# Six of eleven feed-forward blocks by seven products in place of five, without a pause between them

## The chip, the cores and the metric

The kernel runs on one core of a Trainium2 chip. The metric is the device time of one execution in microseconds. The engines are TensorE (PE), VectorE (DVE), ScalarE (ACT) and GpSimd (POOL); SyncE (SP) here only issues DMAs.

## The reference, cut to what matters

Three layers run one after the other on 256 tokens of width 2048, each with its norm and its mixer, all in float32. The change touches the feed-forward part of the first layer, of hidden width 5632:

```
h2 = rms_norm(x, norm2_g)                                   # 256 x 2048
x = x + (silu(h2 @ w_gate) * (h2 @ w_up)) @ w_down          # 2048 x 5632 twice, 5632 x 2048
```

## The kernel before

Float32 products are made from three matmuls each: an operand is split into a rounded part `hi` (a cast on ScalarE, L162) and the rest `lo` (a subtraction on VectorE, L163), and `three` (L186 to L189) multiplies hi by hi, hi by lo and lo by hi. Every weight tile (128 x 2 x 512, 512 KB) is loaded, split, and used once. `raw` tiles have five buffers, `hi` and `lo` four each.

The hidden width is cut into 11 blocks of 512. A block is done in one of two ways:

- `plain(j)`: `linear` for w_gate, then for w_up, each 8 weight tiles against the whole of h2; silu on the first, the scaling and product at L556, then `act_done`: transposes on TensorE (`tr`, L545) and a split, which leave the block's activations in the form that the down product multiplies with.
- `seven(j)`: a scheme with seven products of half-size matrices in place of eight. It queues 28 side pieces in `side`. A piece loads a tile, forms what it multiplies, splits it, and issues 6 matmuls (`times`). The first 12 pieces (`first`: three products) take raw tiles as loaded; the later 16 (`rest`: four products, b5, b7, b6 and b4) take differences of block tiles, made at L668 on VectorE. Block tiles (`b`, and two `u` units) live in a ring of six buffers and are loaded by `ahead` one step before they are used. The last piece calls `last`: additions on VectorE (L676 to L682) that combine the products, silu (L297, L298), two scalings (L685), and `act_done`.

The side pieces run between the matmuls of the main work. After each `three` of a `linear`, `deal` counts one, and when `pace[0]` deals have passed it issues the next piece. `down(bs, last)` multiplies the activations of blocks `bs` by w_down, four column blocks of 512 one after the other, and adds each into x on VectorE (`x_add`, L254, two additions).

Before, plain block 0 comes first, then five rounds, each with one seven block queued beside one plain block and one down call of two blocks; `drain` issues what is left of the queue at the end of each round. All weight loads are issued by SP (`rows`, L126), in one queue. A scheduler puts each engine's instructions in a fixed order when the kernel is built; at run time each engine takes its own in that order and waits on semaphores.

Of the kernel before, what the change touches and what calls it, by code (L numbers as in the profile page):

```python
# [18 lines left out]
P = 128  # L19
# [61 lines left out]
def model(ctx, tc, a, out):  # L81
    nc = tc.nc
# [14 lines left out]
    def nm(s):  # L97
        cnt[0] += 1
        return f"{s}{cnt[0]}"
# [4 lines left out]
    def unit(i, shape, dtype=F32):  # L104
        return wk.tile([P] + list(shape), dtype, tag=f"u{i}", name=nm(f"u{i}_"))
# [15 lines left out]
    def raw_tile():  # L121
        return raw_p.tile([P, 2, 512], F32, tag="raw", name=nm("raw"))

    def rows(dst, w, k, c0, n=512):

        nc.sync.dma_start(dst[:, :, :n], w[k * P:(k + 2) * P, c0:c0 + n].rearrange("(k p) f -> p k f", p=P))  # L126

    def fetch(w, kg, c0, n):

        raws = [raw_tile() for _ in range(2)]  # L130
        for i in range(2):
            rows(raws[i], w, 4 * kg + 2 * i, c0, n)
        return raws
# [26 lines left out]
    def split(hi, lo, src, scale=None):  # L160
        if scale is None:
            A.copy(hi, src)  # L162
            V.tensor_tensor(lo, src, hi.bitcast(F32), ALU.subtract)  # L163
        else:
            A.activation(hi, src, AF.Copy, scale=scale)
            V.scalar_tensor_tensor(lo, src, scale, hi.bitcast(F32), ALU.mult, ALU.subtract)
# [9 lines left out]
    side = deque()  # L176
    pace = [1, 0]

    def deal():
        if side:  # L180
            pace[1] += 1
            if pace[1] >= pace[0]:
                pace[1] -= pace[0]
                side.popleft()()

    def three(o, xh, xl, hi, lo, start, stop):  # L186
        T.matmul(o, xh, hi, start=start, stop=False)  # L187
        T.matmul(o, xh, lo, start=False, stop=False)  # L188
        T.matmul(o, xl, hi, start=False, stop=stop)  # L189

    def linear(w, c0, n, groups, got=(), fine=False):
        accs = [ps_acc.tile([P, 512], F32, tag="acc", name=nm("acc")) for _ in range(2)]
        for gi, ((xh, xl), kg) in enumerate(groups):
            raws = got[gi] if gi < len(got) else fetch(w, kg, c0, n)
            for k in range(4):
                k2 = k % 2
                if k2 == 0:
                    raw = raws[k // 2]
                    hi = hl_p.tile([P, 2, 512], F32R, tag="hi", name=nm("hi"))
                    lo = hl_p.tile([P, 2, 512], F32R, tag="lo", name=nm("lo"))  # L200
                    if fine and gi == 0:
                        for j in range(2):
                            split(hi[:, j, :n], lo[:, j, :n], raw[:, j, :n])
                    else:
                        split(hi[:, :, :n], lo[:, :, :n], raw[:, :, :n])
                for t in range(2):
                    o = accs[t][:, :n]
                    st, en = gi == 0 and k == 0, gi == len(groups) - 1 and k == 3
                    sl = slice(t * P, (t + 1) * P)
                    three(o, xh[:, k, sl], xl[:, k, sl], hi[:, k2, :n], lo[:, k2, :n], st, en)  # L210
                    deal()
        return accs
# [35 lines left out]
    def full(st):  # L248
        return [(st["T"][b], b) for b in range(4)]

    def x_add(b, accs):
        for t in range(2):
            xs = x[:, t, b * 512:(b + 1) * 512]
            V.tensor_tensor(xs, xs, accs[t], ALU.add)  # L254
# [61 lines left out]
    for b in range(4):  # L316
        xh, xl = st["T"][b] = pair(xt_p, "x")
# [13 lines left out]
    got = first  # L331
    for c0, n in ((2688, 400), (2304, 384), (2048, 256)):
        accs = linear(w_in, c0, n, full(st), got, fine=n == 400)
        got = []
# [91 lines left out]
    for vb in range(2):  # L426
# [4 lines left out]
        for hh in range(2):  # L431
# [19 lines left out]
            for t in range(2):  # L451
                o = po[:, t * S:(t + 1) * S]
                T.matmul(o, aT[:, t], v[:, t, vs], start=True, stop=True)
                for c in range(2):
                    n = 2 * t + c
# [69 lines left out]
    w_gate, w_up, w_down = a["w_gate"][0], a["w_up"][0], a["w_down"][0]  # L525
# [3 lines left out]
    acts = {}  # L529
    nst = new_stream()  # L530

    def down(bs, last):
        for b in range(4):
            x_add(b, linear(w_down, b * 512, 512, [(acts[j], j) for j in bs]))
            if last:
                x_done(nst, b, NEV)

    def act_done(j, sg):
        ah, al = acts[j] = pair(mt_p, "m")
        for i in range(2):  # L540
            ps = ps_w.tile([P, 512], F32, tag="w", name=nm("tr"))
            for k in range(2):
                for t in range(2):
                    c = (2 * i + k) * P
                    T.transpose(ps[:, k * S + t * P:k * S + (t + 1) * P], sg[:, t, c:c + P], ident)  # L545
            split(ah[:, 2 * i:2 * i + 2].rearrange("p c s -> p (c s)"),
                  al[:, 2 * i:2 * i + 2].rearrange("p c s -> p (c s)"), ps)

    def plain(j):
        ag = linear(w_gate, j * 512, 512, full(st))  # L550
        sg = unit(4, [2, 512])
        for t in range(2):
            silu_gate(sg[:, t], ag[t], rh[:, t:t + 1])
        au = linear(w_up, j * 512, 512, full(st))
        for t in range(2):
            V.scalar_tensor_tensor(sg[:, t], au[t], r2h[:, t:t + 1], sg[:, t], ALU.mult, ALU.mult)  # L556
        act_done(j, sg)

# [63 lines left out]
    def work_bank():  # L624
        return ps_w.tile([P, 512], F32, tag="w", name=nm("at"))

    def seven(j):

        c0 = j * 512
        c = {}  # L630

        def first(kp, n):
            if kp == 0:
                c[n] = work_bank()
            raw = raw_tile()
            rows(raw, (w_gate, w_up, w_gate)[n], (0, 8, 8)[n] + 2 * kp, c0)
            times(c[n], ("A11", "S4", "A12")[n], parts(raw), kp)
            if n == 2:
                ahead(0, kp)
            if kp < 3:  # L640
                return
            if n < 2:
                c["p", n] = temp("Lx", 4)
                A.copy(c["p", n], c[n])
                return
            sg = c["sg"] = unit(5, [2, 512])
            c11 = temp("junk2", 3)
            V.tensor_tensor(c11, c["p", 0], c[2], ALU.add)
            silu_gate(sg[:, 0], c11, rh[:, 0:1])

        def ahead(kp, n):

            if kp > 3:
                return
            for i in ((0, 1), (), (2,), (3,))[n]:
                b = c["b", kp, i] = block_tile()
                rows(b, (w_up, w_gate, w_up, w_gate)[i], (0, 0, 8, 8)[i] + 2 * kp, c0)

        def rest(kp, n):
            ahead(kp + 1, n)  # L660
            if n == 0:
                if kp == 0:
                    pace[0] = 5.75
                    c["P"] = [work_bank() for _ in range(3)] + [ps_acc.tile([P, 512], F32, tag="acc", name=nm("acc"))]
            b12, b11, b22, b21 = [c["b", kp, i] for i in range(4)]
            dst, x0, x1, which = ((b11, b12, b11, "S1"), (b12, b22, b12, "S3"), (b22, b22, b11, "S2"),
                                  (b21, b22, b21, "A22"))[n]
            V.tensor_tensor(dst, x0, x1, ALU.subtract)  # L668
            times(c["P"][n], which, parts(dst), kp)
            if kp == 3 and n == 3:  # L670
                last()

        def last():
            b5, b7, b6, b4 = c["P"]
            p1, p3, sg = c["p", 0], c["p", 1], c["sg"]
            V.tensor_tensor(p1, p1, b6, ALU.add)  # L676
            c12, c21 = temp("junk2", 3), temp("junk2", 3)
            V.tensor_tensor(c12, p1, b5, ALU.add)
            V.tensor_tensor(p1, p1, b7, ALU.add)
            V.tensor_tensor(c21, p1, b4, ALU.subtract)  # L680
            V.tensor_tensor(p1, p1, b5, ALU.add)
            V.tensor_tensor(c12, c12, p3, ALU.add)  # L682
            silu_gate(sg[:, 1], c21, rh[:, 1:2])
            for t, cu in enumerate((c12, p1)):
                V.scalar_tensor_tensor(sg[:, t], cu, r2h[:, t:t + 1], sg[:, t], ALU.mult, ALU.mult)  # L685
            act_done(j, sg)


        pace[0] = 1.75
        side.extend([lambda kp=kp, n=n: first(kp, n) for kp in range(4) for n in range(2)])  # L690
        side.extend([lambda kp=kp: first(kp, 2) for kp in range(4)])
        side.extend([lambda kp=kp, n=n: rest(kp, n) for kp in range(4) for n in range(4)])

    def drain():
        while side:
            side.popleft()()
        pace[0] = 1

    plain(0)
    left_sums()  # L700
    for w in range(5):
        seven(2 * w + 1)
        plain(2 * w + 2)
        down([2 * w - 1, 2 * w + 2] if w else [0, 2], False)
        drain()
    down([9], True)
    st = nst
    r, rh, r2 = stats(st)

# [72 lines left out]
    for half in range(2):  # L782
# [15 lines left out]
        for c in range(4):  # L798
            i = 4 * half + c
# [202 lines left out]
    for g in range(4):  # L1002
# [4 lines left out]
        sg = unit((0, 4)[g % 2], [2, 512])  # L1007
# [53 lines left out]
```

## Time and profile before

| | |
|---|---|
| three timed runs | 1927.04, 1927.17, 1930.02 us; median 1927.17 |
| the profiled execution | 1926.19 us, its span 1924.4 us |
| busy share of the span | PE 99%, DVE 66%, ACT 50%, POOL 10% |
| granted TensorE clock | 1.00 of full speed |
| feed-forward stage | about 446 to 1140 us of the span |

Times in the views count from the start of the span. A matmul's listed time includes its way through the array, so that neighbours overlap; the step from start to start is what one costs. In brackets behind a row stands the time for which the engine stood idle before it, and what ended that.

### The profile page before, as it was taken

The numbers are of one execution on the slowest core, as the hardware profiler recorded it, in microseconds if no ns is written. First come the engines' busy times: TensorE is split into PE (matmuls) and PEld (weight loads), VectorE is DVE, ScalarE is ACT, GpSimd is POOL, SyncE is SP. The second block draws the span as 40 slices with busy tenths as digits, with TensorE's granted clock in tenths as the row PEclk, the third lists the DMA queues.
The fourth block names the chain that finished last, engine by engine and source line by source line (L and its number), as shares of the span: only waits on it lengthen the run. The fifth ranks groups of instructions, "written<-read, shape, count | busy, mean of one in ns | idle before, by whom it ended". The sixth has DMA issues, their size and how long they took to land.

```text
span 1924.4 us, 23805 instructions
## 1 busy us (share of the span) xinstructions
PE 1906.0 (99%) x8808; PEld 1567.0 (81%) x8808; DVE 1276.6 (66%) x1486; ACT 968.9 (50%) x1313; POOL 201.1 (10%) x315
## 2 busy tenths in 40 slices
PE   8999999999999999999999999999999999999999
PEld 8877888888778888788787888888888888878787
DVE  6454555587787887787887875555555666677654
ACT  6544545465546546455455454444444354566542
POOL 1000222110000000000000110100000003754100
PEclk9999999999999999999999999999999999999999
DMA  8675665567768778677687656566666556544464
GB/s 306 198 209 152 186 175 165 166 207 249 247 223 276 233 227 272 221 259 240 229 268 238 191 165 192 159 196 169 191 188 191 191 179 188 170 132 132 146 202 134
DMA packets 202724, 387.72 MB, mean 201 GB/s; under 512 B 12312, under 2 KB 20528, under 8 KB 202480
## 3 DMA queue, kind: packets, MB, share of 16 engines
q1 hardware_dynamic: 201472, 382.12, 64.3%
q0 software_dynamic: 992, 4.03, 0.7%
q8 instruction: 69, 1.13, 0.2%
q14 instruction: 47, 0.39, 0.1%
q10 hardware_dynamic: 144, 0.05, 0.0%
HBM read 384.04 MB, written 3.68 MB: 201 GB/s over the span
## 4 chain that ended last, share of the span: by engine, by line
PE 89%; DMA 4%; DVE 4%; issue 1%; POOL 1%; ACT 0%; SPq 0%; DVEq 0%; ACTq 0%
PE acc L188 25%; PE acc L187 25%; PE acc L189 25%; PE at L188 2%; PE at L189 2%; PE at L187 2%; DVE lo L163 2%; DMA b<-in_w_up_dram 2%; DMA b<-in_w_gate_dram 1%; PE at L960 1%; DVE b L668 1%; DMA u<-in_w_up_dram 1%; PE tr L225 1%; PE tr L307 1%; DMA u<-in_w_gate_dram 0%
## 5 line engine op out<-in xcount | busy, mean ns | idle before, releaser
L163 DVE TENSOR_TENSOR lo<-raw,hi 128x1024 fp32r<-128x1024 f32 (+3 forms) x646 | 786.4, 1224 | 464.8 <-ACT hi L162 460.2
L162 ACT CAST hi<-raw 128x1024 fp32r<-128x1024 f32 (+3 forms) x646 | 669.4, 1040 | 664.8 <-PE acc L189 561.5
L188 PE MATMUL acc<-lo,xh 128*128 128x512 f32 (+3 forms) x1640 | 637.2, 389 | 0.4 <-DVE lo L163 0.4
L189 PE MATMUL acc<-hi,xl 128*128 128x512 f32 (+3 forms) x1640 | 636.2, 388 | 0.0
L187 PE MATMUL acc<-hi,xh 128*128 128x512 f32 (+3 forms) x1640 | 622.7, 390 | 5.7 <-ACT hi L162 5.7
L187 PEld LDWEIGHTS acc<-hi,xh 128*128 128x128 f32 x1640 | 308.2, 188 | 68.8 <-ACT hi L162 6.0
L188 PEld LDWEIGHTS acc<-lo,xh 128*128 128x128 f32 x1640 | 308.9, 188 | 64.1 <-issue 3.3
L189 PEld LDWEIGHTS acc<-hi,xl 128*128 128x128 f32 x1640 | 309.0, 188 | 59.5 <-issue 0.4
L188 PE MATMUL acc<-lo,mh 128*128 128x512 f32 x640 | 251.0, 392 | 0.0
L189 PE MATMUL acc<-hi,ml 128*128 128x512 f32 x640 | 249.0, 393 | 0.0
L187 PE MATMUL acc<-hi,mh 128*128 128x512 f32 x640 | 247.1, 393 | 1.0 <-ACT mh L162 1.0
L187 PEld LDWEIGHTS acc<-hi,mh 128*128 128x128 f32 x640 | 120.5, 188 | 27.1 <-DVE x L254 1.5
L188 PEld LDWEIGHTS acc<-lo,mh 128*128 128x128 f32 x640 | 120.3, 188 | 25.7 <-DVE lo L163 1.8
L189 PEld LDWEIGHTS acc<-hi,ml 128*128 128x128 f32 x640 | 119.8, 188 | 24.4
L162 ACT CAST hi<-b 128x1024 fp32r<-128x1024 f32 x54 | 56.9, 1054 | 74.5 <-PE acc L189 47.3
L163 DVE TENSOR_TENSOR lo<-b,hi 128x1024 fp32r<-128x1024 f32 x54 | 65.9, 1221 | 4.8 <-ACT hi L162 3.9
L668 DVE TENSOR_TENSOR b<-b,b 128x1024 f32<-128x1024 f32 x41 | 50.1, 1222 | 28.3 <-DMA b<-in_w_gate_dram 13.5
L720 POOL DMA_DIRECT2D u<-in_c_even_dram x1 | 0.6, 633 | 651.9 <-PE at L189 651.9
L254 DVE TENSOR_TENSOR x<-x,acc 128x512 f32<-128x512 f32 x88 | 57.7, 681 | 9.9 <-PE acc L189 9.8
L188 PE MATMUL at<-lo,u 128*128 128x512 f32 x160 | 63.5, 397 | 0.4 <-DVE lo L163 0.3
L189 PE MATMUL at<-hi,u 128*128 128x512 f32 x160 | 62.4, 390 | 0.0
L187 PE MATMUL at<-hi,u 128*128 128x512 f32 x160 | 62.4, 390 | 0.0
(253 smaller groups left out, 1567.1 us busy)
## 6 DMA issues: line engine op xcount, KB each, us to landing
raw<-in_ev_w_in_dram SPq DMA_DIRECT2D x128, 512.0 KB, 3.9
raw<-in_w_gate_dram SPq DMA_DIRECT2D x88, 512.0 KB, 4.5
raw<-in_w_down_dram SPq DMA_DIRECT2D x88, 512.0 KB, 5.1
raw<-in_w_in_dram SPq DMA_DIRECT2D x80, 512.0 KB, 3.8
raw<-in_od_w_in_dram SPq DMA_DIRECT2D x72, 512.0 KB, 3.7
raw<-in_w_up_dram SPq DMA_DIRECT2D x68, 512.0 KB, 4.7
raw<-in_w_out_dram SPq DMA_DIRECT2D x32, 512.0 KB, 3.6
raw<-in_ev_w_out_dram SPq DMA_DIRECT2D x32, 512.0 KB, 3.7
```

Of the source, the lines that this page charges most:

```text
L162: A.copy(hi, src)
L163: V.tensor_tensor(lo, src, hi.bitcast(F32), ALU.subtract)
L187: T.matmul(o, xh, hi, start=start, stop=False)
L188: T.matmul(o, xh, lo, start=False, stop=False)
L189: T.matmul(o, xl, hi, start=False, stop=stop)
L225: T.transpose(ps[:, k * S + t * P:k * S + (t + 1) * P], x[:, t, c:c + P], ident)
L254: V.tensor_tensor(xs, xs, accs[t], ALU.add)
L307: T.transpose(ps[:, k * S + t * P:k * S + (t + 1) * P], src(t)[:, c:c + P], ident)
L668: V.tensor_tensor(dst, x0, x1, ALU.subtract)
L720: nc.gpsimd.dma_start(ce, a["c_even"][:, :512])
L960: T.matmul(pv[e * 64:(e + 1) * 64, :S], vo[:, k, g * 64:(g + 1) * 64], PT[:, :, e], start=k == 0, stop=k == t)
```

## The change

The six seven blocks are 1, 3, 5, 7, 9 and 10; 0, 2, 4, 6 and 8 stay plain. All six are queued at once after block 0, and side pieces run on without a drain between them, at pace 1.5 in the first 12 pieces of a block and 4.85 in its later 16 (4.1 for block 1), where 1.75 and 5.75 stood; `drain` comes once, before the last down call. There are seven down calls in place of six. Block tiles are loaded by GpSimd's queue, in program order. `plain` hands back its `act_done`, which is called by `linear` behind the first group of the next down call's first column block (`mid`). Lines move by 3 up to `plain` (L163 stays, L254 becomes L257, L298 L301, L545 L548, L556 L559) and by 6 in `seven` (L668 becomes L674, L676 to L682 become L682 to L688, L685 L691).

```diff
-    def rows(dst, w, k, c0, n=512):
+    def rows(dst, w, k, c0, n=512, queue=nc.sync):
-        nc.sync.dma_start(dst[:, :, :n], w[k * P:(k + 2) * P, c0:c0 + n].rearrange("(k p) f -> p k f", p=P))
+        return queue.dma_start(dst[:, :, :n], w[k * P:(k + 2) * P, c0:c0 + n].rearrange("(k p) f -> p k f", p=P))
...
     def deal():
         if side:
             pace[1] += 1
-            if pace[1] >= pace[0]:
+            while side and pace[1] >= pace[0]:
                 pace[1] -= pace[0]
                 side.popleft()()
...
-    def linear(w, c0, n, groups, got=(), fine=False):
+    def linear(w, c0, n, groups, got=(), fine=False, mid=None):
         accs = [ps_acc.tile([P, 512], F32, tag="acc", name=nm("acc")) for _ in range(2)]
-        for gi, ((xh, xl), kg) in enumerate(groups):
+        for gi, (pr, kg) in enumerate(groups):
+            if gi == 1 and mid is not None:
+                mid()
+            xh, xl = pr() if callable(pr) else pr
...
-    def down(bs, last):
+    def down(bs, last, mid=None):
         for b in range(4):
-            x_add(b, linear(w_down, b * 512, 512, [(acts[j], j) for j in bs]))
+            x_add(b, linear(w_down, b * 512, 512, [(lambda j=j: acts[j], j) for j in bs], mid=mid if b == 0 else None))
...
-        act_done(j, sg)
+        return lambda: act_done(j, sg)
...
             if kp == 0:
+
+                pace[0] = 1.5
                 c[n] = work_bank()
...
-                rows(b, (w_up, w_gate, w_up, w_gate)[i], (0, 0, 8, 8)[i] + 2 * kp, c0)
+                tc.keep_in_program_order(rows(b, (w_up, w_gate, w_up, w_gate)[i], (0, 0, 8, 8)[i] + 2 * kp, c0,
+                                              queue=nc.gpsimd))
...
-                    pace[0] = 5.75
+                    pace[0] = 4.85 if j > 1 else 4.1
...
-        pace[0] = 1.75
...
-    plain(0)
+    plain(0)()
     left_sums()
-    for w in range(5):
-        seven(2 * w + 1)
-        plain(2 * w + 2)
-        down([2 * w - 1, 2 * w + 2] if w else [0, 2], False)
-        drain()
-    down([9], True)
+    for j in (1, 3, 5, 7, 9, 10):
+        seven(j)
+    mid = plain(2)
+    down([0], False)
+    mid()
+    down([2, 1], False)
+    for j in (4, 6, 8):
+        mid = plain(j)
+        down([j - 1, j], False, mid)
+    down([9], False)
+    drain()
+    down([10], True)
```

SP's order before, where the up product of plain block 2 is loaded; `raw` tiles of w_up belong to it, `b` tiles to block 1, which runs beside it:

```order
L126 DMA raw852_4141<-in_w_up_dram 128x2x512
L126 DMA raw863_4202<-in_w_up_dram 128x2x512
L126 DMA b860_4189<-in_w_gate_dram 128x2x512
L126 DMA raw864_4203<-in_w_up_dram 128x2x512
L126 DMA raw873_4253<-in_w_up_dram 128x2x512
L126 DMA b855_4157<-in_w_up_dram 128x2x512
L126 DMA raw874_4254<-in_w_up_dram 128x2x512
L126 DMA b869_4232<-in_w_up_dram 128x2x512
```

The same place of SP's order after:

```order
L126 DMA raw858_4167<-in_w_up_dram 128x2x512
L126 DMA raw869_4228<-in_w_up_dram 128x2x512
L126 DMA raw870_4229<-in_w_up_dram 128x2x512
L126 DMA raw881_4290<-in_w_up_dram 128x2x512
L126 DMA raw882_4291<-in_w_up_dram 128x2x512
L126 DMA raw893_4352<-in_w_up_dram 128x2x512
```

And the first block loads in GpSimd's order after, with nothing between them:

```order
L126 DMA b811_3973<-in_w_up_dram 128x2x512
L126 DMA b812_3975<-in_w_gate_dram 128x2x512
L126 DMA b819_4010<-in_w_up_dram 128x2x512
L126 DMA b827_4038<-in_w_gate_dram 128x2x512
L126 DMA u10_830_4048<-in_w_up_dram 128x2x512
```

The block loads have left the places between raw loads and are a sequence of their own.

TensorE's order before, where the transposes of a plain block (`tr`, L545) stand; `mh` and `ml` are activations in a down product (accumulator `acc`), `at` a product of the seven block:

```order
L188 MATMUL acc1325_6410<-lo1332_6433,mh1175_5720 128x512
L189 MATMUL acc1325_6410<-hi1331_6432,ml1176_5721 128x512
L187 MATMUL at1262_6098<-hi1335_6444,u3_763_3789 128x512
L545 MATMUL tr1323_6396<-cm_90,u4_1276_6163 128x128
L187 MATMUL acc1326_6411<-hi1329_6416,mh1175_5720 128x512
L188 MATMUL acc1326_6411<-lo1330_6417,mh1175_5720 128x512
```

And after, at a plain block's transposes in a later down product:

```order
L188 MATMUL at1384_6580<-lo1477_7044,u2_761_3785 128x512
L189 MATMUL at1384_6580<-hi1476_7043,u8_762_3786 128x512
L548 MATMUL tr1480_7064<-cm_90,u4_1421_6771 128x128 x4
L187 MATMUL at1385_6581<-hi1486_7093,u2_761_3785 128x512
L188 MATMUL at1385_6581<-lo1487_7094,u2_761_3785 128x512
```

Four transposes stand together now, later in the down product, among a side piece's matmuls.

VectorE's order before at the end of block 1, from the first addition of `last` up to its first scaling; `at836` is product b6, `lo` tiles from `raw` belong to the down product:

```order
L676 TENSOR_TENSOR c802_3944<-c802_3944,at836_4070 128x512
L163 TENSOR_TENSOR lo970_4739<-raw967_4734,hi969_4738 128x1024
L678 TENSOR_TENSOR c959_4694<-c802_3944,at834_4068 128x512
L163 TENSOR_TENSOR lo972_4755<-raw968_4735,hi971_4754 128x1024
L679 TENSOR_TENSOR c802_3944<-c802_3944,at835_4069 128x512
L682 TENSOR_TENSOR c959_4694<-c959_4694,c806_3961 128x512
L254 TENSOR_TENSOR x_91<-x_91,acc939_4595 128x512
L668 TENSOR_TENSOR b1047_5081<-b1046_5079,b1047_5081 128x1024
L254 TENSOR_TENSOR x_91<-x_91,acc940_4596 128x512
L163 TENSOR_TENSOR lo976_4775<-raw973_4770,hi975_4774 128x1024
L685 SCALAR_TENSOR_TENSOR u5_830_4053<-c959_4694,r2h694_3443,u5_830_4053 128x512
```

And after, the same end of block 1 (`at834` is b6 there), up to the lo tile lo959 of the down product that follows; the first scaling comes two rows later:

```order
L682 TENSOR_TENSOR c800_3931<-c800_3931,at834_4054 128x512
L163 TENSOR_TENSOR lo942_4591<-raw930_4532,hi941_4590 128x1024
L163 TENSOR_TENSOR lo946_4601<-raw944_4598,hi945_4600 128x1024
L684 TENSOR_TENSOR c935_4554<-c800_3931,at832_4052 128x512
L674 TENSOR_TENSOR b1011_4865<-b1010_4863,b1011_4865 128x1024
L163 TENSOR_TENSOR lo950_4620<-raw948_4617,hi949_4619 128x1024
L163 TENSOR_TENSOR lo953_4635<-raw951_4632,hi952_4634 128x1024
L685 TENSOR_TENSOR c800_3931<-c800_3931,at833_4053 128x512
L688 TENSOR_TENSOR c935_4554<-c935_4554,c804_3951 128x512
L257 TENSOR_TENSOR x_91<-x_91,acc927_4529 128x512
L257 TENSOR_TENSOR x_91<-x_91,acc928_4530 128x512
L163 TENSOR_TENSOR lo959_4653<-raw956_4648,hi958_4652 128x1024
```

More lo subtractions of 1024 elements stand between the additions than before: those of the next seven block's first products (lo946, lo950, lo953) have joined the down product's.

## Rows read from the trace of the kernel before

**Rows 1.** The page, engines: busy us, share of the span, instructions.

```profile
PE 1906.0 (99%) x8808; PEld 1567.0 (81%) x8808; DVE 1276.6 (66%) x1486; ACT 968.9 (50%) x1313; POOL 201.1 (10%) x315
```

**Rows 2.** Windows: stretch, length, engines' busy us; then PE clock, DMA share, GB/s.

```profile
446.00:1140.00 694.00, 687.27 (x3065) 561.98 (x3064) 554.43 (x556) 369.29 (x400) 12.18 (x30) 1.00 0.74 237
...
590.00:618.00 28.00, 28.00 (x125) 23.19 (x124) 19.63 (x18) 17.33 (x18) 0.00 (x0) 1.00 0.91 295
```

**Rows 3.** Timeline of PE, two neighbours: start us, us, engine, line, operation.

```profile
565.57 0.39 PE L188 MATMUL at<-lo,u 128*128 128x512 f32 x1
565.80 0.39 PE L189 MATMUL at<-hi,u 128*128 128x512 f32 x1
```

**Rows 4.** Waits, 446 to 1140: us in all, times, longest; then PE's timeline.

```profile
PE tr L545 <- DVE u L556: 5.3, 4, 1.9
...
528.14 0.39 PE L187 MATMUL at<-hi,u 128*128 128x512 f32 x1
530.48 0.33 PE L545 MATMUL tr<-cm,u 128*128 128x128 f32 x1 [1.95 <-DVE u L556]
```

**Rows 5.** Timeline of DVE at two plain blocks' scalings.

```profile
528.53 1.23 DVE L668 TENSOR_TENSOR b<-b,b 128x1024 f32<-128x1024 f32 x1 [3.29 <-DMA b<-in_w_gate_dram]
529.67 1.40 DVE L556 SCALAR_TENSOR_TENSOR u<-acc,r2h,u 128x512 f32<-128x512 f32 x2
...
785.09 1.23 DVE L668 TENSOR_TENSOR b<-b,b 128x1024 f32<-128x1024 f32 x1 [2.98 <-DMA b<-in_w_gate_dram]
```

**Rows 6.** Waits, 446 to 1140, of DVE and of SP's queue.

```profile
DVE b L668 <- DMA b<-in_w_gate_dram: 13.2, 5, 3.3
...
SPq L126 <- DVE lo L163: 540.0, 304, 6.9
```

**Rows 7.** Timeline of DVE at the end of block 1.

```profile
563.57 1.23 DVE L668 TENSOR_TENSOR u<-b,u 128x1024 f32<-128x1024 f32 x1 [2.39 <-DMA b<-in_w_up_dram]
...
570.51 0.68 DVE L676 TENSOR_TENSOR c<-c,at 128x512 f32<-128x512 f32 x1
571.11 1.22 DVE L163 TENSOR_TENSOR lo<-raw,hi 128x1024 fp32r<-128x1024 f32 x1
572.24 0.68 DVE L678 TENSOR_TENSOR c<-c,at 128x512 f32<-128x512 f32 x1
...
578.78 0.74 DVE L685 SCALAR_TENSOR_TENSOR u<-c,r2h,u 128x512 f32<-128x512 f32 x1
579.44 0.68 DVE L680 TENSOR_TENSOR c<-c,acc 128x512 f32<-128x512 f32 x1
```

**Rows 8.** Timeline of PE, block 1's first transposes.

```profile
581.77 0.38 PE L545 MATMUL tr<-cm,u 128*128 128x128 f32 x2
```

**Rows 9.** Timeline of POOL and DVE, issues and operations of POOL.

```profile
1072.80 0.55 POOL L721 DMA_DIRECT2D u<-in_c_even_dram  x1
1072.86 1.23 DVE L163 TENSOR_TENSOR lo<-raw,hi 128x1024 fp32r<-128x1024 f32 x1 [0.36 <-ACT hi L162]
...
1083.89 1.23 DVE L163 TENSOR_TENSOR lo<-raw,hi 128x1024 fp32r<-128x1024 f32 x1
1084.11 1.20 POOL L839 TENSOR_TENSOR tabs<-co__9133 128x64 f32<-128x64 f32 x1
...
1085.69 0.32 POOL L839 TENSOR_TENSOR tabs<-co__9133 128x64 f32<-128x64 f32 x1
1085.76 0.69 DVE L679 TENSOR_TENSOR c<-c,at 128x512 f32<-128x512 f32 x1
```

**Rows 10.** DMA issues, 446 to 1140: count, KB each, median us to landing.

```profile
raw<-in_w_down_dram SPq DMA_DIRECT2D x88, 512.0 KB, 5.1
...
b<-in_w_gate_dram SPq DMA_DIRECT2D x25, 512.0 KB, 4.7
...
u<-in_c_even_dram POOLq DMA_DIRECT2D x1, 512.0 KB, 5.1
...
co__9133<-in_od_sinks_dram POOLq DMA_DIRECT2D x1, 16.0 KB, 5.3
```

## The prediction

> **What bounds the kernel now.** I read the engine table first: TensorE is busy 1906.0 of 1924.4 us, VectorE 66%, ScalarE 50% [rows 1]. A gain has to come from fewer matmuls or from TensorE's few idle microseconds, and nothing else can shorten the span. The windows view then separates the feed-forward stage from the rest: in its 694 us TensorE is busy 687.27 and VectorE 554.43, or 80%, at granted clock 1.00; in a stretch where a seven block's first products run, the DMA share is 0.91 at 295 GB/s [rows 2]. So VectorE and the DMA engines are the ones with little left there, ScalarE is not (369 of 694).
>
> The timeline of TensorE gives the unit of the sum. Three 512-column matmuls start 0.227 us apart, though each is listed with 0.39, since they are pipelined [rows 3]. The view of waits names where the stage's idle time sits: TensorE waits 5.3 us in four places for the scaling at L556, in front of a plain block's activation transposes (L545) [rows 4]. From start to start each place loses 0.16 more (0.39 less 0.227), so 5.3 + 4 x 0.16 = 5.9 us.
>
> Why the scaling is late stands in VectorE's timeline: it stood 3.29 us at L668, a seven block's subtraction, until a block tile of w_gate had landed, and only then came to L556; 257 us later the same stands there with 2.98 [rows 5]. Block tiles land late because SP's queue issues in order: it waits 540.0 us in 304 places for a raw buffer that VectorE must finish with, and block loads stand behind those waits [rows 6].
>
> **The change part by part.** *Fewer matmuls.* A plain block has two products of 4 groups x 4 slices x 2 row halves x 3 = 192 matmuls; a seven block 7 x 8 x 3 = 168. Block 10 changes kind: 24 x 0.227 = 5.4 us less on TensorE, which sets the end. The number of down matmuls is the same.
>
> *Transposes moved.* In the changed order 25 to 54 matmuls (at least 5.6 us) stand between the up product's last matmul and the plain transposes, where 18 (4.1 us) stood. A stall like that of rows 5 fits under them, all the more if block tiles come earlier. I take all 5.9 us as gained; the other end is none of it, if VectorE's stall grows by as much.
>
> *Block loads on GpSimd's queue.* 96 loads (80 before) leave SP and are alone on their queue through the stage, in program order; SP's raw loads no longer have them in between. Each waits only for its own buffer, which the order frees four side pieces or more ahead: a piece is 4.85 x 3 + 6 = 20.6 matmuls, 4.66 us, so 18.6 us ahead, and at pace 4.1 16.6 us. A 512 KB load from GpSimd landed in 5.1 us, a block load from SP in 4.7 [rows 10]. That leaves 11.5 us to spare, so I price this at nothing; what hides it is the ring of six tiles, and without that cover each late load would stop VectorE as in rows 5. Issuing costs GpSimd 0.55 us, and one such issue lay under a running lo subtraction without growing [rows 9].
>
> GpSimd's tensor operations do suffer beside VectorE: the same operation took 0.32 us beside L679, which reads PSUM, and 1.20 beside a lo subtraction, whose operands all lie in SBUF [rows 9]. The Trainium skill (SBUF — State Buffer, "SBUF: two separate sides") has a rule against this part of the change: while VectorE runs a two-port operation, GpSimd cannot write the descriptors of its own DMAs, and a load of about 0.62 us took about 3.1. By that rule, an estimate from the page's two figures, each load would come 2.5 us later; within 11.5 us of spare the sum would be the same, and only if VectorE leaves no gaps would it be rival D. The one issue of rows 9 that lies beside VectorE does not show the rule.
>
> *Six blocks without a pause.* A seven block's VectorE work is 28 lo subtractions and 16 block subtractions at 1.13 us, and about 13 short ones at 0.60 to 0.66, together 58 us; a plain block's is 16 x 1.13 + 6 short = 22 us (pitches from rows 7). One block more of the first kind, one less of the second, and 8 residual adds of the seventh down call give 36 + 5 = 41 us: 595 in some 690, 86%. While block 1's later products run (pace 4.1, down of one block) a piece holds 2.27 + 1.16 + 0.6 = 4.0 us of VectorE work in 4.15 us. That covers nothing that comes late, so the ends of the six seven blocks decide.
>
> *Block ends.* When the last matmul of product b6 is done, VectorE runs L676 and its followers, and TensorE transposes what the two scalings (L685) leave. Before, 11 operations, 4 of them long, go up to the first scaling: 7 x 0.61 + 4 x 1.13 = 8.8 us, and TensorE has 68 matmuls (15.4 us) until its transposes: 6.6 us over. The trace agrees: L676 began 4.3 us after the matmul that began at 565.80 had ended, since VectorE had waited 2.39 us for a block tile just before; the scaling ended at 579.52, and the transposes began at 581.77, without a wait [rows 7, 8].
>
> After, the pieces come closer and the down products' own subtractions and residual adds stand among the same operations. For block 1 the order puts 12 operations (6 long) up to lo959, which TensorE wants 33 matmuls after b6: 10.4 us of work against 7.5 us. The same count for the others, work up to the scaling against matmuls up to its transposes: block 3, 9.3 against 42 (9.5 us); block 5, 11.7 against 43 (9.8); block 7, 10.0 against 58 (12.7); block 9, 9.3 against 42 (9.5); block 10, second scaling, 14.3 against 68 (15.2). The balances are -2.9, +0.2, -1.9, +2.7, +0.2 and +0.9.
>
> Something comes on top of each: the last matmul's 0.39 us, 0.07 from the scaling to the transposes, and the rest of the operation VectorE is in, half of 1.13. That is 1.1 us, and with it TensorE waits 4.0 + 0.9 + 3.0 + 0 + 0.9 + 0.2 = **9.0 us**. Bounds: nothing, if the scheduler's places leave more room than my count; and 26.6 us (7.2 + 4.1 + 6.2 + 1.6 + 4.1 + 3.4), if VectorE gets to L676 4.3 us late as in rows 7. I take a value near the low end, because the cause of those 4.3 us, a block load behind SP's waits, is what moves.
>
> *First products' pace.* At 1.5 in place of 1.75 a piece takes 10.5 matmuls, not 11.25, so the demand goes from 295 to 303 GB/s and the DMA share from 0.91 to about 0.93. Raw loads still fit; their failure is in D. Outside the stage the order hardly moves: no cost.
>
> Sum against the profiled execution's 1926.2: -5.4 - 5.9 + 9.0 = 1923.9. That execution is 1.0 below the median of the three runs (1927.17), so on the runs' scale I say **1925 us**. A measurement of this kernel can tell 0.2% (3.9 us) from no change.
>
> **Rivals.** *B, block ends cost nothing.* For it: before, the same ends had 2.2 us left over even with VectorE 4.3 us late. Against it: five of six counts have under 1 us of spare. Time: 1926.2 - 11.3 = 1914.9, 1916 on the runs' scale.
>
> *C, VectorE becomes the bound at the ends (slower).* It reaches L682 (the former L676) about 4.3 us after b6 at each end, because at 86 to 97% load it no longer runs ahead. Place: the transposes at L548 and the first down matmuls after them. Price 26.6 us, so 1926.2 - 11.3 + 26.6 = 1941.5, 1942 on the runs' scale. It decides the sign as soon as the ends cost more than 11.3 us together, 1.9 us each. For it: the load; against it: in the old order VectorE's waits for block loads, not its load, made the lateness.
>
> *D, the new queue does not help.* GpSimd's loads come late, or take DMA time from SP's raw loads in the stretches at 0.91, where four block loads and the first products' raw loads overlap. If two queues halve the rate there, a raw load of 5.1 us takes 2.5 more at each of six phases: +15, so 1938.9, 1940 on the runs' scale. For it: a 16 KB load from GpSimd took 5.3 us, no less than 512 KB [rows 10]. Against it: 11.5 us of spare. The rule on descriptors named above would give this case its cause.
>
> **How the numbers follow.** My forecast (ends cost 5 to 15 us) 0.57; B 0.18; C 0.14; D 0.11. The forecast's own range is 1921 to 1931. Faster by over 0.2% means under 1923.3: all of B and about a third of the forecast (ends under 7.5 us), 0.38. Slower, over 1931.0: nearly all of C, most of D, 0.22. The rest, 0.40, is within. The range runs from B at its least, 1915, up to 1935, which leaves out C and D at full price, less than 2 in 10 after what falls short of it.
>
> **What would show it.** Right: TensorE's matmul count 24 lower at the same clock; no wait of L548 on L559 (the former L556); new waits of L548 on L691 (the former L685) and of L188 on lo near blocks 1 and 5, 3 to 4 us each; VectorE's waits for block tiles (13.2 us for one kind in rows 6) mostly gone. Wrong: waits at all six ends over 3 us (C); VectorE still waiting for block DMAs, or GpSimd loads landing in over 8 us (D); no wait over 1 us at any end (B). The step I trust least is the 1.1 us.

## The result, and the profile after

The changed kernel takes 1971.25 us (median of four runs, 1968.65 to 1978.41), against 1927.11 for the kernel before: slower by the factor 1.0235 (95% interval 1.0221 to 1.0249). I had said 1925 us, 1915 to 1935.

The engine table of the profiled execution, which answers to [rows 1]:

```profile
span 1966.9 us, 23847 instructions
...
PE 1914.1 (97%) x8784; PEld 1566.1 (80%) x8784; DVE 1316.3 (67%) x1529; ACT 983.4 (50%) x1327; POOL 275.8 (14%) x411
```

The span is 42.5 us longer. TensorE's idle time went from 18.4 us to 1966.9 - 1914.1 = 52.8, so 34.4 us are waits. The other 8.1 are longer busy time with 24 matmuls fewer; as those took 5.4 us with them, the matmuls that are left cost 13.5 us more. The windows view shows a part of that, here around the end of block 1 (columns as in [rows 2]):

```profile
560.00:570.00 10.00, 5.06 (x20) 3.36 (x18) 10.00 (x12) 3.15 (x3) 0.00 (x0) 0.91 0.70 211
570.00:580.00 10.00, 9.06 (x35) 7.02 (x36) 7.10 (x9) 3.40 (x5) 0.00 (x0) 0.75 0.39 115
580.00:590.00 10.00, 10.00 (x49) 8.34 (x48) 9.45 (x11) 7.41 (x10) 0.00 (x0) 1.00 0.79 265
```

The timeline of TensorE at the same place:

```profile
569.76 0.80 PE L187 MATMUL acc<-hi,mh 128*128 128x512 f32 x1 [2.73 <-DVE x L257]
571.49 0.79 PE L188 MATMUL acc<-lo,mh 128*128 128x512 f32 x1 [0.94 <-DVE lo L163]
572.08 0.63 PE L189 MATMUL acc<-hi,ml 128*128 128x512 f32 x1
572.51 0.63 PE L188 MATMUL acc<-lo,mh 128*128 128x512 f32 x1
```

TensorE waits again and again from 560 to 571 us, busy 5.06 of 10, while VectorE is busy all 10.00. After it the granted clock falls to 0.75 as a mean of the next 10 us: the last two matmuls start 0.43 us apart, not 0.227 [rows 3], so they run at the lower of the clock's two levels, 1.2 and not 2.4 GHz. By 580 it is whole again. The granted clock is at half like this in four stretches of the execution, the first of them ahead of the feed-forward stage:

```profile
431.60:435.10 3.50, 3.46 (x8) 2.78 (x9) 3.50 (x4) 1.04 (x1) 0.00 (x0) 0.51 0.50 150
568.10:575.00 6.90, 4.31 (x9) 3.10 (x10) 6.55 (x10) 0.72 (x1) 0.00 (x0) 0.51 0.68 222
684.20:691.10 6.90, 5.29 (x14) 4.23 (x15) 5.53 (x8) 1.76 (x2) 0.00 (x0) 0.51 0.73 228
899.20:906.10 6.90, 5.02 (x12) 3.96 (x13) 6.90 (x8) 1.04 (x1) 1.44 (x2) 0.51 0.43 115
```

TensorE is busy for 18.08 us of them, and half of that, 9.0 us, is the most that the clock can have cost. The rest of the 13.5 us is mainly, by my estimate, the 0.16 us that a wait costs beyond its length (0.39 less 0.227): TensorE has 42 waits over the span, where it had 10, which makes some 5 us.

The view of waits says for what TensorE waits in the stage (us in all, times, longest):

```profile
PE acc L188 <- DVE lo L163: 16.8, 23, 1.7
PE tr L548 <- DVE u L691: 5.3, 3, 2.8
PE at L188 <- DVE lo L163: 5.0, 3, 4.3
PE acc L187 <- DVE x L257: 3.7, 2, 2.7
```

The view of line L674 (L668 before) says until what VectorE stood idle ahead of block subtractions (us, times):

```profile
  DMA b<-in_w_up_dram: 30.6, 15
  DMA b<-in_w_gate_dram: 21.4, 10
  DMA u<-in_w_up_dram: 21.0, 8
  DMA u<-in_w_gate_dram: 12.0, 6
```

TensorE waits for VectorE in these four rows, the largest, and for lo tiles most of all. And VectorE waits 85.0 us in 39 places for block tiles. The same view of the kernel before adds up to 59.4 in 29, so these waits are not new; there are more of them, each hardly longer (2.2 us on average, 2.0 before), and now they cost. How one of them comes about stands in the timelines of GpSimd and VectorE:

```profile
526.46 0.72 POOL L126 DMA_DIRECT2D b<-in_w_up_dram  x1 [6.13 <-DVE lo L163]
...
527.22 1.22 DVE L163 TENSOR_TENSOR lo<-u,hi 128x1024 fp32r<-128x1024 f32 x1
533.14 1.22 DVE L674 TENSOR_TENSOR b<-b,b 128x1024 f32<-128x1024 f32 x1 [4.70 <-DMA b<-in_w_up_dram]
```

GpSimd's queue waits until VectorE's lo subtraction has read the buffer, issues at 526.46, and VectorE arrives at the subtraction that needs the new tile at 528.4, before it can have landed. It stands there 4.70 us, and all plain lo tiles queue behind it.

### The profile page after: what moved, and what is told of

It is laid out like the page before. It is cut to its first block, busy times and chain, and to the rows that moved or that the text cites. A ratio compares the mean times of both kernels' runs of the same rounds, so it can differ in the third digit from the quotient of the medians.

```text
span 1966.9 us, 23847 instructions
## 1 busy us (share of the span) xinstructions
PE 1914.1 (97%) x8784; PEld 1566.1 (80%) x8784; DVE 1316.3 (67%) x1529; ACT 983.4 (50%) x1327; POOL 275.8 (14%) x411
## 4 chain that ended last, share of the span: by engine, by line
PE 73%; issue 9%; DVE 8%; DMA 7%; POOL 2%; ACT 1%; SPq 0%; DVEq 0%; POOLq 0%; ACTq 0%
PE acc L188 20%; PE acc L189 20%; PE acc L187 20%; DVE lo L163 5%; DMA b<-in_w_gate_dram 3%; PE at L187 2%; PE at L188 2%; PE at L189 2%; DMA u<-in_w_gate_dram 1%; DMA b<-in_w_up_dram 1%; DMA u<-in_w_up_dram 1%; POOL b L126 1%; DVE b L674 1%; PE at L970 1%; PE tr L310 1%
## 5 line engine op out<-in xcount | busy, mean ns | idle before, releaser
L163 DVE TENSOR_TENSOR lo<-raw,hi 128x1024 fp32r<-128x1024 f32 (+3 forms) x642 | 781.8, 1224 | 448.6 <-ACT hi L162 445.8
L188 PE MATMUL acc<-lo,xh 128*128 128x512 f32 (+3 forms) x1584 | 616.4, 389 | 8.4 <-DVE lo L163 8.3
L189 PE MATMUL acc<-hi,xl 128*128 128x512 f32 (+3 forms) x1584 | 615.4, 389 | 2.9 <-DVE xl L166 2.9
L187 PE MATMUL acc<-hi,xh 128*128 128x512 f32 (+3 forms) x1584 | 603.8, 390 | 7.6 <-ACT hi L162 7.6
L188 PEld LDWEIGHTS acc<-lo,xh 128*128 128x128 f32 x1584 | 298.5, 188 | 72.7 <-DVE lo L163 14.2
L189 PEld LDWEIGHTS acc<-hi,xl 128*128 128x128 f32 x1584 | 298.5, 189 | 61.4 <-DVE xl L166 3.3
L162 ACT CAST hi<-b 128x1024 fp32r<-128x1024 f32 x64 | 67.5, 1054 | 64.8 <-PE acc L189 57.3
L163 DVE TENSOR_TENSOR lo<-b,hi 128x1024 fp32r<-128x1024 f32 x64 | 78.2, 1223 | 6.4 <-ACT hi L162 5.8
L674 DVE TENSOR_TENSOR b<-b,b 128x1024 f32<-128x1024 f32 x48 | 58.6, 1221 | 34.5 <-DMA b<-in_w_gate_dram 21.4
L188 PE MATMUL at<-lo,u 128*128 128x512 f32 x192 | 76.0, 396 | 5.0 <-DVE lo L163 5.0
L189 PE MATMUL at<-hi,u 128*128 128x512 f32 x192 | 75.2, 392 | 0.0
L187 PE MATMUL at<-hi,u 128*128 128x512 f32 x192 | 75.2, 392 | 0.0
L257 DVE TENSOR_TENSOR x<-x,acc 128x512 f32<-128x512 f32 x96 | 62.5, 681 | 9.1 <-PE acc L189 9.0
L126 POOL DMA_DIRECT2D b<-in_w_up_dram x32 | 23.2, 725 | 296.7 <-DVE lo L163 296.7
```

The lines of the kernel that those rows point to most:

```text
L126: return queue.dma_start(dst[:, :, :n], w[k * P:(k + 2) * P, c0:c0 + n].rearrange("(k p) f -> p k f", p=P))
```

## Theories

**L, late tiles.** VectorE's order puts block subtractions far ahead of the places where their results are needed, and so ahead of the landing of their tiles. VectorE then stands still with everything queued behind it, and the schedule without pauses leaves it no time to catch up. In the printed order of the changed kernel a subtraction stands 14 rows ahead of its split (median; 17 before); one of the widest cases is this one at the end of block 1, where the tile belongs to block 3 (row numbers ahead):

```
384 L674 TENSOR_TENSOR u11_994_4794<-u10_993_4792,u11_994_4794 128x1024
...
433 L163 TENSOR_TENSOR lo1017_4873<-u11_994_4794,hi1016_4872 128x1024
```

**V, load.** VectorE's work in the dense pieces is too much for any order (rival C's reason). **Q, queue.** GpSimd's queue is the cause (rival D).

## The experiments

**Queue and parts alone.** The changed kernel with block loads on SP's queue:

```diff
-                tc.keep_in_program_order(rows(b, ..., c0, queue=nc.gpsimd))
+                rows(b, ..., c0)
```

> The changed kernel with its block loads back on SP's queue. In the changed kernel VectorE waits 77.5 us for block tiles in the feed-forward stage (59 before) and TensorE loses 44.7 us waiting, 8.2 before. Theory L (late tiles: block subtractions stand in VectorE's order earlier than their tile can land, whichever queue loads it, and VectorE has no time left to make the stall good): SP's loads land 0.5 to 2 us sooner after their buffer comes free, so part returns, 1945 to 1965 us. Rival Q (GpSimd's queue is the cause): 1915 to 1930. Rival V (VectorE's load alone starves TensorE, block tiles do not matter): 1965 to 1975.

Measured 1971.46 us, ratio to before 1.0221 (1.0204 to 1.0238): nothing comes back, a miss of theory L's range and inside V's, and Q falls for this schedule. VectorE's waits for tiles are 78.4 us here, and ahead of the same line it stands another 10.3 us, in five places, for which the view names no end. The reverse, the kernel before with only its block loads on GpSimd's queue:

> The kernel before with only the block loads moved to GpSimd's queue, in program order. Theory L: VectorE's waits for block tiles grow a little, and with five blocks and drains VectorE makes most of it good: 1927 to 1942 us. Rival Q: 1950 to 1965, most of the 44 us. Rival V: 1922 to 1928, and SP's raw loads rather sooner.

Measured 1954.81 us, 1.0136 (1.0109 to 1.0163). So the queue alone costs 27 us in the old schedule, more than theory L's range allows and inside Q's. The view of the subtractions' line (L669 here) shows by what:

```profile
  DMA b<-in_w_up_dram: 32.5, 13
  DMA b<-in_w_gate_dram: 31.3, 11
  DMA u<-in_w_up_dram: 22.1, 6
  DMA u<-in_w_gate_dram: 16.1, 7
```

102.0 us in place of 59.4. Either edit lengthens or uncovers the same waits, and their costs don't add up (27 from the queue, 44 with or without it in the new schedule).

The kernel before with only the transposes moved (`mid` in `linear` and `down`, and `return lambda: act_done(j, sg)`, as in the change):

> The kernel before with only the activation transposes of a plain block moved into the next down product. If the 5.9 us that TensorE loses in front of them are gained as the prediction took it: 1920 to 1923 us. If the stall only moves on to the next operand that VectorE makes: 1925 to 1928.

Measured 1928.72 us, 1.0008 (0.9997 to 1.0018): no gain. TensorE's largest wait in the stage shows where the 5.9 us went:

```profile
PE acc L187 <- DVE u L559: 7.6, 5, 2.1
```

The timelines of VectorE and TensorE at one of the five places:

```profile
527.19 1.23 DVE L671 TENSOR_TENSOR b<-b,b 128x1024 f32<-128x1024 f32 x1 [3.19 <-DMA b<-in_w_gate_dram]
528.33 1.40 DVE L559 SCALAR_TENSOR_TENSOR u<-acc,r2h,u 128x512 f32<-128x512 f32 x2
...
529.13 0.50 PE L187 MATMUL acc<-hi,mh 128*128 128x512 f32 x1 [1.34 <-DVE u L559]
```

The late scaling also reads the accumulators of the up product, and TensorE now waits for it before a down product's first matmul, which writes an accumulator. The stall had two takers, and the change removed one.

**Pauses.** The changed kernel with five seven blocks (block 10 plain) and SP's queue:

```diff
-    for j in (1, 3, 5, 7, 9, 10):
+    for j in (1, 3, 5, 7, 9):
...
-                    pace[0] = 4.85 if j > 1 else 4.1
+                    pace[0] = 5.75 if j > 1 else 4.1
...
-    down([9], False)
-    drain()
-    down([10], True)
+    mid = plain(10)
+    drain()
+    down([9, 10], True, mid)
```

> The changed kernel with five seven blocks as before (block 10 is plain), paces 1.5 and 5.75 (4.1 in block 1) and loads on SP's queue; what stays of the change is the queue without pauses, the other order of the down calls and the moved transposes. If the sixth block and its paces make the loss (rival V): 1925 to 1935 us. If running on without a pause makes it, since subtractions can then be put up to a block ahead of their place (theory L): 1945 to 1970.

Measured 1959.39 us, 1.0164 (1.0145 to 1.0183), in theory L's range. With the old number of blocks, the old queue and the old later pace, 32 of the 44 us stay: they don't need the sixth block. This run still has the other order of down calls and the moved transposes in it. A purer test of the pause, though not a pure one, changes one number of the kernel before:

```diff
-                    pace[0] = 5.75
+                    pace[0] = 6.65
```

> The kernel before with one number changed: pace 6.65 in place of 5.75 in the later products, so that a seven block's pieces fill a round's 128 deals (113 before) and no stretch without side pieces is left at a round's end. VectorE has the same work, less of it in each microsecond. If the quiet stretch is where VectorE makes its waits for late tiles good (theory L, and the reason why the schedule without pauses loses even with five blocks): slower, 1932 to 1955 us. If density decides (rival V): 1920 to 1929.

Measured 1955.59 us, 1.0141 (1.0124 to 1.0158), just above theory L's range. At the old pace a round ended with 15 deals, some 45 matmuls or 10 us, without side pieces. Spreading the same work over them makes VectorE's load smaller at each moment and costs 27 us. TensorE's largest waits in the stage:

```profile
PE acc L187 <- DVE x L254: 8.3, 5, 2.1
PE at L188 <- DVE lo L163: 8.1, 4, 2.4
PE acc L188 <- DVE lo L163: 4.4, 10, 0.6
```

The kernel before has none of these three above 0.5 us. That is against V. But the number moves more than the pause: in VectorE's printed order a subtraction now stands 22 rows ahead of its split (median; 17 before), and VectorE's waits for tiles grow from 59.4 to 73.7 us. So the run shows that the old schedule rested on its pace and its quiet stretch together; what the stretch alone is worth is not shown.

**The place of the subtractions.** The changed kernel with each subtraction kept behind the instruction ahead of it in the program, which puts it right before its split:

```diff
-            V.tensor_tensor(dst, x0, x1, ALU.subtract)
+            tc.keep_in_program_order(V.tensor_tensor(dst, x0, x1, ALU.subtract))
```

> The changed kernel with each block subtraction kept behind the VectorE instruction that stands ahead of it in the program, so that the scheduler can't put it earlier. The same work, queue and paces. Theory L: VectorE's waits for block tiles fall from 77.5 to under 15 us and TensorE's idle time from 44.7 to under 12: 1918 to 1932 us. Rival V: the load is the same, 1955 to 1975. Rival Q: GpSimd's loads stay as slow, 1955 to 1975.

Measured 1987.82 us, 1.031 (1.0295 to 1.0325), slower still, and outside every range given. No wait for a block tile is left, but the view of ScalarE's waits shows a new chain:

```profile
ACT hi L162 <- DVE b L674: 167.9, 61, 4.2
ACT hi L162 <- DVE u L674: 71.2, 26, 4.1
```

Subtraction, cast, lo subtraction and matmuls now follow one another with nothing between. By itself this run speaks rather for V than for L; it shows only that this place is wrong too. So the subtraction was written one side piece ahead of its split, in a function `minus` of its own (its body, the lines moved into it, is left out here; it keeps the subtraction in program order):

```diff
-            V.tensor_tensor(dst, x0, x1, ALU.subtract)
-            times(c["P"][n], which, parts(dst), kp)
+            times(c["P"][n], which, parts(dst), kp)
...
+                minus(kp + n // 3, (n + 1) % 4)
...
             silu_gate(sg[:, 0], c11, rh[:, 0:1])
+            minus(0, 0)
```

> The changed kernel with each block subtraction written one side piece ahead of its split and kept there. Pinned right before the split, the subtractions no longer waited for tiles, but ScalarE's casts then waited 245 us for the subtractions. Theory L (late tiles in an order that comes too early; the remedy is a place between the two): waits for tiles under 20 us, casts waiting for subtractions under 30, TensorE idle under 15 us: 1918 to 1935 us. Rival V (VectorE's load in the dense pieces is too high for any order): 1950 to 1990.

Measured 1951.51 us, 1.0127 (1.0112 to 1.0142). The same in the kernel before:

> The kernel before with the same rearrangement: each block subtraction one side piece ahead of its split and kept there, loads on SP's queue. Theory L: VectorE's 59 us of waits for tiles go, and with them TensorE's waits for the scalings, 5.9 us: 1918 to 1924 us. Rival V: nothing to gain at 80% load, 1925 to 1929, or slower if casts wait for subtractions.

Measured 1952.21 us, 1.0131 (1.0116 to 1.0146). Both are misses of theory L. Both have one place, which the timelines of the first of them show, TensorE's two rows ahead and VectorE's behind:

```profile
483.93 0.39 PE L189 MATMUL at<-hi,xl 128*128 128x512 f32 x1
488.87 0.79 PE L187 MATMUL at<-hi,u 128*128 128x512 f32 x1 [4.55 <-ACT hi L162]
...
484.36 0.69 DVE L653 TENSOR_TENSOR c<-c,at 128x512 f32<-128x512 f32 x1 [3.81 <-PE at L189]
485.83 0.69 DVE L301 SCALAR_TENSOR_TENSOR u<-u,c 128x512 f32<-128x512 f32 x1 [0.79 <-ACT u L300]
486.44 1.22 DVE L683 TENSOR_TENSOR b<-b,b 128x1024 f32<-128x1024 f32 x1
```

I had put a block's first subtraction (L683 at 486.44) behind the addition L653, which waits for TensorE's last matmul of a product; TensorE then waits for the subtraction's cast. One line was moved:

```diff
+            minus(0, 0)
             sg = c["sg"] = unit(5, [2, 512])
...
             silu_gate(sg[:, 0], c11, rh[:, 0:1])
-            minus(0, 0)
```

> As the run with subtractions one piece ahead (1951.5 us), but a block's first subtraction stands ahead of the addition L653 that waits for product matmuls, not behind it. In that run TensorE's waits were 4.7 us at four of the six changes from first to later products and 2.0 at two, 0.7 more behind the four, and half clock for some 2 us after the long ones. Theory L (VectorE's order is all of it): these 26 us go, and about 8 of clock with them: 1914 to 1922 us, faster than before. Rival V (load): VectorE's waits only move, 1930 to 1950.

Measured 1914.67 us, 0.9931 (0.9919 to 0.9944), in theory L's range. The kernel before in the same order:

> The kernel before with the same order of subtractions. Theory L: 1952 less 27 us of these waits and 7 of clock, 1916 to 1922 us, below 1927.5 because the 5.9 us in front of the transposes go too. Then the sixth block's 5.4 us are what the changed schedule has over this one. Rival V: 1925 to 1940.

Measured 1915.19 us, 0.9936 (0.9924 to 0.9949), just under theory L's range. And the first of these with SP's queue:

> The first kernel of this group with its block loads on SP's queue. If, with the subtractions in place, only order matters and a tile's landing does not: within 2 us of that kernel. If SP's waits for raw buffers make block tiles late: 5 to 20 us slower than it. If GpSimd's queue is the worse: 5 us faster.

Measured 1913.51 us, 0.993 (0.9916 to 0.9943). No wait for a block tile is left in any of the three. The queue, which cost 27 us in the old schedule with its old order, makes no difference that can be measured in the new schedule once tiles have time to land. Last, two pieces ahead:

```diff
-                minus(kp + n // 3, (n + 1) % 4)
+                minus(kp + n // 2, (n + 2) % 4)
...
             minus(0, 0)
+            minus(0, 1)
```

> The fast version with loads on GpSimd's queue (1914.7 us, each subtraction one side piece ahead of its split), but two pieces ahead. In VectorE's order a subtraction then stands 6 rows ahead of its split (median); it was 3 at one piece ahead, 14 in the changed kernel, 1 where it was pinned to its split. Theory L: one tile in four now has one piece (4.7 us) between its load's issue and its subtraction, less than the 5.3 us of landing, so VectorE waits for tiles again, 15 to 50 us in all, and the time is 1917 to 1945 us. If the place does not matter as long as it is fixed: 1912 to 1917.

Measured 1910.88 us, 0.9909 (0.9893 to 0.9926), the fastest version; my expectation of new waits was wrong. The stage's window:

```profile
440.00:1130.00 690.00, 687.92 (x3089) 568.30 (x3088) 604.07 (x607) 388.09 (x418) 82.00 (x120) 1.00 0.77 251
```

And all of TensorE's waits in it:

```profile
PE acc L187 <- ACT hi L162: 1.1, 1, 1.1
PE acc L187 <- ACT mh L162: 0.8, 1, 0.8
PE acc L188 <- DVE lo L163: 0.2, 1, 0.2
```

VectorE is busy 604.07 of 690 us, 88% (80% in [rows 2]), and TensorE hardly waits. The load that V holds to be too much is as high as in the run before it (604.28 us in the same window) and far above the changed kernel's 567.82 of 694, and this is the fastest run of all. Of what the second piece of distance gains, the waits show this much: ScalarE's casts wait 53.7 us for subtractions at one piece ahead and 11.2 at two. Theory L stands, with one correction: a subtraction can also stand too late. Places 1 row ahead of the split (1987.82), 3 (1914.67) and 6 (1910.88) and the scheduler's 14 (1971.25) all carry the same work and the same queue. The rows alone don't decide: the run at 1951.51 us differs from the one at 1914.67 only in the place of a block's first subtraction, behind or ahead of an addition that waits for TensorE.

## Why the prediction was wrong

*The step that failed* is the price of nothing for block loads, with 11.5 us to spare. It counted from a buffer's release to the side piece that uses the tile, but what uses the tile first is VectorE's subtraction, and the order had that up to 12 pieces and more ahead of its own. The spare was none: VectorE stood 85.0 us for tiles, and more than a third of the loads were what a subtraction waited for (39 of 96), in the kernel before too (29 of 80), as [rows 5, 7] already showed with 3.29, 2.98 and 2.39 us. I read these as the fault of SP's queue, which the change would mend. That reading is the deeper error: where the queue was exchanged and the order kept, the waits grew from 59.4 to 102.0 us; where the order was changed and the queue kept, they were gone.

*Block ends, 9.0 us.* The count of operations was sound (41 us more for VectorE, 39.7 by the engine tables); the allowance, 1.1 us by which VectorE comes late to the first addition, hung on the same reading. At block 1's end the last matmul of b6 and that addition stand so in the timelines:

```profile
555.18 0.39 PE L189 MATMUL at<-hi,u 128*128 128x512 f32 x1
...
560.95 0.68 DVE L682 TENSOR_TENSOR c<-c,at 128x512 f32<-128x512 f32 x1
```

That is 5.4 us late; the other five ends, read in the same way, have 4.1, 2.8, 2.5, 4.7 and 0.9. The windows from b6's last matmul to the block's first transposes (the first of the six, and the sum) show what TensorE lost there:

```profile
555.18:575.50 20.32, 13.37 (x44) 9.01 (x43) 19.47 (x24) 5.27 (x6) 0.72 (x1) 0.83 0.66 211
...
sum 94.44, PE 74.71 PEld 55.97 DVE 92.47 ACT 36.08 POOL 3.61; mean PE 12.45 PEld 9.33 DVE 15.41 ACT 6.01 POOL 0.60
```

It was idle for 94.44 - 74.71 = 19.7 us, twice my 9.0. So rival C's place came about, for some half of the stage's 36.8 us of idle time (694.00 less 657.23 busy), and three quarters of its 26.6 us. Its reason, the load, did not. In the run at two pieces ahead, under the higher load and without late tiles, the same place reads:

```profile
545.54 0.39 PE L189 MATMUL at<-hi,u 128*128 128x512 f32 x1
...
546.84 0.68 DVE L690 TENSOR_TENSOR c<-c,at 128x512 f32<-128x512 f32 x1
```

That is 0.9 us late, and all six ends lie between 0.7 and 1.1. The allowance fits a kernel whose tiles are in time; I took the changed kernel for one.

*Transposes, -5.9 us.* Alone this part gained nothing: I followed the scaling's one reader and missed that its operands, the accumulators, were waited for as well.

*Fewer matmuls, -5.4 us.* The count fell by 24, as said. What the sixth block is worth when the order is right can be read from 1914.67 and, with SP's queue, 1913.51 against 1915.19: the intervals overlap. TensorE's busy time there is 1897.5 and 1896.3 us against 1901.1, so 3.6 to 4.8 of the 5.4 us came, and its idle time is 15.6 and 14.8 us against 12.9, which takes 2.7 and 1.9 of that back.

*What no step had.* TensorE's longer busy time, 13.5 us: at most 9.0 of clock, and for most of the rest what each wait costs beyond its length. And the pause: I took the stretch without side pieces for spare room to be filled, while filling it at pace 6.65 cost 27 us. With the subtractions in place the schedule without pauses loses nothing (1910.88 to 1914.67 us), so the pause mattered to an order with late tiles; that VectorE caught up in it is argued from this, and not measured by itself.

*Rival D and GpSimd's queue.* Landing times of the changed kernel:

```profile
raw<-in_w_gate_dram SPq DMA_DIRECT2D x80, 512.0 KB, 4.7
...
b<-in_w_up_dram POOLq DMA_DIRECT2D x30, 512.0 KB, 5.2
b<-in_w_gate_dram POOLq DMA_DIRECT2D x30, 512.0 KB, 5.4
```

A block load takes 5.1 to 5.4 us from GpSimd, by kind, where the same kinds took 4.7 to 4.9 from SP in the kernel before: 0.3 to 0.7 more, at a VectorE load above 80%. By my estimate from the rule of the Trainium skill that I weighed (SBUF — State Buffer, "SBUF: two separate sides") it would have been 2.5 us more. That page of the Trainium skill has its two figures from a copy on VectorE, and VectorE's work here is subtractions of two tiles, so I should not have carried them over. Nearer is a table of the Trainium skill (DMA: Bandwidth & Descriptors, "Latency and other measured facts"), with a first byte after about 1 us from GpSimd's queue and 0.6 from SP's: a difference of 0.4, with which the trace agrees. That this is what cost 27 us in the kernel before with GpSimd's queue is not shown: there one kind of load (`u` of w_gate, 13 loads) landed in 6.5 us, 1.8 more than from SP, and why was not taken apart.

*Open.* SP's queue in the new schedule is no faster than GpSimd's, although its waits for tiles seem 6.6 us less (78.4 against 85.0); with the 10.3 us for which the view names no end they are 88.7, no less at all. It was not tried at how many pieces ahead tiles begin to come late again, nor whether a ring of more than six block tiles would do what the new order does.

## What to carry to other kernels

A load's slack ends at the instruction that first touches the tile in its engine's order, not at the product for which it is loaded; print that order before pricing a load at nothing. An in-order engine that waits for a DMA holds up everything behind it, and if it does so in the old kernel without harm, look for the room that covers it before filling that room. Where a scheduler puts work too early, write the operation one or two steps ahead of its use and keep it there: here that alone took the kernel before from 1927 to 1915.19 us and the changed kernel from 1971 to 1914.67 and 1910.88, while in the same order the change that was being made gained nothing that can be told from no change (1914.67 against 1915.19).

## What was unexpected of the hardware

The price of stalls beyond their length: after some 10 us in which TensorE was about half busy (5.06 of 10.00), its matmuls started 0.43 us apart in place of 0.227 for a few microseconds. Another such stretch (899 to 906) begins during a single wait, the one of 4.3 us in the view of waits. Over the execution the clock came to at most 9.0 us, and with what each wait costs on top of its length to 13.5, about a third of the loss of 42.5. In the run at two pieces ahead the granted clock of the whole stage is 1.00.
